# Layer 1 of a two-layer hybrid backbone entered by token tiles, low halves of weights moved in VectorE's order, step size sums in two runs

## The chip, the cores and the metric

The kernel runs on one core of a Trainium2 chip. The metric is the device time of one launch in microseconds, as the median of several runs.

## What is computed

The reference passes 256 latent tokens of width 2048 (and 256 context tokens) through two layers; everything is float32.

```
# layer 0: neighbourhood attention (16 heads of 128) beside a bidirectional SSD scan (8 groups)
shift, scale, gate = split(silu(c) @ ada_w[0] + ada_b[0])
h = rms_norm(x, g[0]) * (1 + scale) + shift          # the context likewise
p = h @ w_in                                         # 2048 x 14400
ya = attention(q, k, v, context) * silu(gate columns)
yb = gated_group_rmsnorm(ssd(x, dt, B, C) + d * x, z)
x = x + gate * (concat(ya, yb) @ w_out)              # 4096 x 2048
# layer 1: short gated convolution
h = rms_norm(x, g[1]) * (1 + scale1) + shift1
bg, cg, hv, g_ = split(h @ sc_w_in)                  # 2048 x 8192
x = x + gate1 * ((silu(g_) * bg * dw_conv(cg * hv)) @ sc_w_out)
```

Inside the scan the step sizes dt are summed along the tokens, forwards and backwards, over the latent tokens (two tiles of 128) and over the context.

## The kernel before

**Products.** Every large product is done in three passes of a shortened float32 format. A weight chunk of 128 x 1024 numbers is loaded into a `raw` buffer. Then `split` (L379) makes two parts of it: ScalarE casts it to the high half wH (L395), and VectorE subtracts that from the weight, which gives the low half wL (L396). There are three wH and three wL buffers, so the chunk that is split takes the place of the one three chunks back. The activations are kept in two parts, too (hH and hL, or one tile h that holds both side by side). TensorE multiplies high by high, low by high and high by low (L188 is the one line of all matmuls, L192 that of all transposes).

**Order.** The instructions of every engine run in the order in which they are written out, and that order is made by a planner at build time. `Plan` (from L38) keeps a modelled time for each engine and each tile. The main program writes TensorE's matmuls in order; after a few of them `pump` looks through three queues of tasks (`urgent`, `side`, `back`). A task is a generator that yields what it needs next (an engine and tiles), and `may` lets it go on once the modelled times say that its inputs are there. `splits_try` writes the next split as soon as the planner takes its weight to have landed, up to three chunks ahead of the one in use; while `hold` is set it writes none, and the queue `back` stands still. `issue` writes the next weight load on SP's queue when a raw buffer is free. A DMA on ScalarE's queue is modelled to end 1500 ns after its transfer.

**Layer 0.** For eight pairs of 128 input columns the modulation (`ada_gen`: products in TensorE, two transposes, the sums L697 to L703 on VectorE) yields h, while keys, values, queries and the first B columns are accumulated by `part_gen` (L749, L751). Then follow the rest of the input projection with attention heads (`head_gen`), the step sizes (`dt_gen`, L1045 to L1136) and the scan (`make_b`, `make_c`, `make_x`, `group_gen`). Meanwhile the task `gemv_gen` in the queue `back` works out further modulation rows on VectorE alone, in pairs of products over a loaded weight (L776).

In `dt_gen` the dt of both streams lies token by token in four blocks of 64 columns (32 heads, two directions). Fourteen matmuls with triangular or all-ones matrices add them up into one bank: running sums of the two latent tiles, their strict sums and totals, and the same for the context.

**Output projection and entry into layer 1.** The output projection goes over 16 chunks of `w_out` (two of the 32 blocks of mixed heads each) for column groups of 512: two groups together, then the third, then the fourth. Each group has a bank for either token tile (`ps[0]`, `ps[1]`), and in every chunk both tiles are multiplied in turn. `res_gen` (from L1491) takes a finished group: for either tile it multiplies the bank by the gate (L1506), adds the residual to give x1a or x1b (L1509) and squares that on ScalarE with a sum along the row (L1511). `turn_gen` (from L1524) transposes x1 block by block (16 blocks of 128 columns, two transposes each, one bank for a block) and scales it on ScalarE on its way to a `late` tile (L1534); blocks 0 to 7 come early, the others once the last group has passed. `norm_gen` (from L1538) starts when all four groups are done: it adds the sums of squares (L1540), takes the power -1/2 of both tiles on GpSimd (L528), builds two diagonal matrices (L1544) and spreads them over the partitions by matmuls into the bank `rb`. Then for each block: the product with `rb` (L1561), the high part on ScalarE (L1563) and the low part on VectorE (L1553). `hold` is set for the last of the 16 chunks of the last group and taken back when block 1 of layer 1 is ready.

**Layer 1.** 16 groups of four banks (`both`, `cg_gen`, `hv_gen`, `bg_gen`, `gg_gen`), each over eight chunks of `sc_in`; then the last projection, four groups of eight chunks of `sc_out`. Its inputs y are made in two parts by `gg_gen` (high L1667, low L1668).

Of the kernel before, what the change touches and what calls it, by code (L numbers as in the profile page):

```python
# [15 lines left out]
KB = 16  # L16
# [21 lines left out]
class Plan:  # L38
# [59 lines left out]
    def add(self, b):  # L98
# [10 lines left out]
        if op == "DMACopy":  # L109
# [4 lines left out]
            if e == "SP":  # L114
                self.dma = max(self.dma, s + 1000) + n / self.RATE
                done = free = self.dma + 1000
            else:
                done = free = max(self.dma, s + 1000) + n / self.RATE + 1500
# [23 lines left out]
def kernel(ctx: ExitStack, tc, x, cx, ada_w, ada_b, w_in, w_out, sc_in, sc_out, rpb, small, const,  # L142
# [96 lines left out]
    def may(task, hor, isurg):  # L239
# [5 lines left out]
        if nb and len(free_b) < nb + (0 if isurg else reserve[0]):  # L245
            return False
        now, t = plan.t["PE"], plan.t["ACT" if eng == "AQ" else eng]
# [130 lines left out]

    def split():  # L379
# [3 lines left out]
        if n == 64:  # L383

            W = WH[k % NW].rearrange("p (b c) -> p b c", b=nb)
# [9 lines left out]
        E(S.copy(H, v))  # L395
        E(V.tensor_tensor(out=Lo, in0=v, in1=H.bitcast(F32), op=ALU.subtract))  # L396
        HL[k] = (H, Lo)
        pos["split"] += 1
        give_raw(raw)
        issue()  # L400

# [17 lines left out]
    def splits_try():  # L419
        if hold[0]:  # L420
            return
        while pos["split"] < pos["use"] + NW and pos["split"] in RAW:
            if plan.ready([RAW[pos["split"]][1]]) > max(plan.t["PE"], plan.t["ACT"]) + 300:
                return
            split()

    def use(ahead=0):
        k = pos["use"] + ahead
        while pos["split"] <= k:
# [4 lines left out]
            split()  # L434
        splits_try()
# [609 lines left out]
    def dt_gen(ps):  # L1045
# [52 lines left out]
        first = True  # L1098
# [32 lines left out]
        E(V.tensor_copy(rw[:64, 0:256], pr[:64, :256]))  # L1131
        E(S.activation(rw[:64, 256:512], pr[:64, :256], AF.Exp))
# [358 lines left out]
    def res_gen(k, c0, ps):  # L1491
# [10 lines left out]
        yield when(lambda: x1 and k in passed)  # L1502
        for t in range(2):
            gb, xr = g2[t]
            yield W_("DVE", ps[t], gb)
# [3 lines left out]
            E(V.tensor_tensor(out=x1[t][:, cols], in0=gb, in1=xr, op=ALU.add))  # L1509
            yield W_("ACT", x1[t][:, cols])  # L1510
            E(S.activation(xr, x1[t][:, cols], AF.Square, accum_out=ss1[:, t, k:k + 1]))  # L1511
            give(free_t, gb, xr)
# [245 lines left out]
```

## Time and profile before

| | us |
|---|---|
| median of 3 runs | 1822.08 |
| lowest and highest | 1821.28, 1822.44 |
| profiled execution | 1820.64 |
| its span, first to last instruction | 1818.9 |
| first TensorE instruction after | 13.8 |
| busy DVE (VectorE) | 1259.2 |
| busy ACT (ScalarE) | 777.4 |

The names in the profile: PE is TensorE's matmuls, PEld its weight loads, DVE is VectorE, ACT ScalarE, POOL GpSimd, SP the queue of loads. A row of the timeline reads: start, length (both us), engine, line, operation, output <- inputs, partitions x elements, count of instructions merged, and in brackets the idle time just before and what ended it. Matmuls overlap, so a row of 0.39 us doesn't mean that the next one waits so long: at full clock the next 512-column matmul starts 0.23 us later. A row of the waits reads: engine, line and tile <- what it waited for: total us, times, longest.

### The profile page before, as it was taken

Reading aid. Unit: us, or ns where it says so; the run is one execution under the profiler, and the core shown is the slowest. Engines: PE = TensorE matmul, PEld = TensorE weight load, DVE = VectorE, ACT = ScalarE, POOL = GpSimd, SP = SyncE. Lnnn points to the kernel's source line nnn. Section 1 sums busy time; section 2 is a strip of 40 time slices with the busy share of each in tenths; the row PEclk is TensorE's granted clock in tenths of the full one; section 3 lists DMA queues with packets and bytes.
Section 4 is the critical chain, followed back from the end, with each engine's and each line's share of the span. In section 5 each row is a group of like instructions: output and inputs, shape, how many; then the busy total and the mean of one; then the engine's idle time right before and its main releaser. Section 6 shows DMA issues by size and latency. Waiting matters only on the chain.

```text
span 1818.9 us, 26339 instructions
## 1 busy us (share of the span) xinstructions
PE 1785.2 (98%) x9959; PEld 1488.2 (82%) x9959; DVE 1259.2 (69%) x2039; ACT 777.4 (43%) x1369; POOL 28.5 (2%) x27
## 2 busy tenths in 40 slices
PE   6999999999999999999999999999999999999998
PEld 4677988888888888888887898788878888888877
DVE  5566785877575877565877677776567777776655
ACT  5323443445232454232444443654444444444442
POOL 0000100000000001000001000000000000000000
PEclk9999999999999999999999999999999999999999
DMA  9997644576565566545575557678676777777665
GB/s 330 334 299 256 203 132 131 167 223 178 169 185 191 154 199 182 192 139 177 163 225 162 169 146 246 206 226 289 220 243 209 222 251 228 231 248 221 186 203 156
DMA packets 249216, 376.90 MB, mean 207 GB/s; under 512 B 32656, under 2 KB 104048, under 8 KB 249088
## 3 DMA queue, kind: packets, MB, share of 16 engines
q1 hardware_dynamic: 239792, 366.64, 65.4%
q10 hardware_dynamic: 9296, 8.57, 1.4%
q8 instruction: 78, 1.28, 0.3%
q14 instruction: 50, 0.41, 0.1%
HBM read 368.70 MB, written 7.77 MB: 207 GB/s over the span
## 4 chain that ended last, share of the span: by engine, by line
PE 84%; issue 8%; DVE 2%; DMA 1%; ACT 1%; POOLq 0%; POOL 0%; SPq 0%; ACTq 0%; DVEq 0%
PE bank L188 82%; PE bank L192 2%; DVE wL L396 1%; DMA raw<-in_ada_w 1%; DMA tmp<-dram_csr 1%; ACT wH L395 0%; DVE tmp L1150 0%; DVE acc L776 0%; DVE h L1553 0%; DVE tmp L1331 0%; DVE hL L725 0%; DVE tmp L1691 0%; DVE tmp L721 0%; DVE tmp L1689 0%; DVE tmp L1334 0%
## 5 line engine op out<-in xcount | busy, mean ns | idle before, releaser
L395 ACT CAST wH<-raw 128x1024 fp32r<-128x1024 f32 (+1 forms) x439 | 458.4, 1046 | 730.4 <-PE bank L188 582.8
L396 DVE TENSOR_TENSOR wL<-raw,wH 128x1024 fp32r<-128x1024 f32 (+1 forms) x439 | 533.0, 1217 | 336.0 <-ACT wH L395 329.6
L188 PE MATMUL bank<-h,wH 128*128 128x512 f32 x1024 | 360.9, 398 | 2.0 <-DVE h L1553 2.0
L188 PE MATMUL bank<-hH,wH 128*128 128x256 f32 (+1 forms) x1040 | 353.4, 340 | 0.8 <-ACT wH L395 0.8
L188 PE MATMUL bank<-hL,wH 128*128 128x256 f32 (+1 forms) x1040 | 338.6, 326 | 0.0
L188 PE MATMUL bank<-hH,wL 128*128 128x256 f32 (+1 forms) x1024 | 331.7, 324 | 0.3 <-DVE wL L396 0.3
L188 PE MATMUL bank<-h,wL 128*128 128x256 f32 x1024 | 286.4, 280 | 0.4 <-DVE wL L396 0.4
L188 PE MATMUL bank<-wH,hH 128*128 128x512 f32 x640 | 257.9, 403 | 3.9 <-ACT hH L719 2.6
L188 PE MATMUL bank<-wL,hH 128*128 128x512 f32 x640 | 250.6, 392 | 0.0
L188 PE MATMUL bank<-wH,hL 128*128 128x512 f32 x640 | 249.7, 391 | 0.1
L188 PEld LDWEIGHTS bank<-h,wH 128*128 128x128 f32 x1024 | 193.0, 188 | 49.6 <-DVE h L1553 2.5
L776 DVE SCALAR_TENSOR_TENSOR acc<-raw,csil,acc 128x512 f32<-128x512 f32 x256 | 191.9, 750 | 42.7 <-DMA raw<-in_ada_w 37.7
L188 PEld LDWEIGHTS bank<-hH,wH 128*128 128x128 f32 x1040 | 196.8, 189 | 24.3 <-issue 7.4
L188 PEld LDWEIGHTS bank<-hL,wH 128*128 128x128 f32 x1040 | 197.1, 190 | 19.7 <-issue 4.8
L188 PEld LDWEIGHTS bank<-hH,wL 128*128 128x128 f32 x1024 | 194.2, 190 | 18.0 <-DVE wL L396 1.0
L188 PEld LDWEIGHTS bank<-h,wL 128*128 128x128 f32 x1024 | 193.5, 189 | 0.7 <-DVE wL L396 0.7
L188 PE MATMUL bank<-wH,mix 128*128 128x512 f32 x512 | 164.1, 396 | 0.3 <-ACT Vt L945 0.3
L188 PEld LDWEIGHTS bank<-wH,hH 128*128 128x128 f32 x640 | 120.2, 188 | 35.4 <-issue 6.2
L188 PEld LDWEIGHTS bank<-wH,hL 128*128 128x128 f32 x640 | 120.2, 188 | 26.3 <-DVE hL L725 0.6
L188 PEld LDWEIGHTS bank<-wL,hH 128*128 128x128 f32 x640 | 120.2, 188 | 24.7 <-DVE wL L409 0.5
L188 PEld LDWEIGHTS bank<-wH,mix 128*128 128x128 f32 x512 | 96.1, 188 | 22.3 <-issue 1.7
L188 PE MATMUL bank<-wL,mix 128*128 128x512 f32 x256 | 99.9, 390 | 0.0
(241 smaller groups left out, 1663.9 us busy)
## 6 DMA issues: line engine op xcount, KB each, us to landing
raw<-in_w_in SPq DMA_DIRECT2D x210, 512.0 KB
raw<-in_ada_w SPq DMA_DIRECT2D x162, 512.0 KB
raw<-in_sc_in SPq DMA_DIRECT2D x128, 512.0 KB
raw<-in_w_out SPq DMA_DIRECT2D x64, 512.0 KB
raw<-in_sc_out SPq DMA_DIRECT2D x32, 512.0 KB
tmp<-dram_csr SPq DMA_DIRECT2D x32, 256.0 KB
PT<-in_ada_w SPq DMA_DIRECT2D x14, 512.0 KB
xtm<-in_ada_w SPq DMA_DIRECT2D x9, 512.0 KB
```

The costliest lines, as they stand in the source:

```text
L188: E(T.matmul(o, l, r, start=start, stop=stop, skip_group_check=True))
L192: E(T.transpose(o, i, ident if k == 128 else ident[:k, :k]))
L395: E(S.copy(H, v))
L396: E(V.tensor_tensor(out=Lo, in0=v, in1=H.bitcast(F32), op=ALU.subtract))
L776: E(V.scalar_tensor_tensor(out=acc, in0=v[:, j], scalar=csil[:, 2 * k + j:2 * k + j + 1], in1=acc, op0=ALU.mult, op1=ALU.add))
```

## The change

1. `split` writes only the cast on ScalarE and puts the low half on a list, `lows`. `low_part` writes the subtraction later: as soon as the planner takes the cast to be done by the time at which VectorE (or TensorE) has come (`lows_try`, which is called ahead of every VectorE task that is let go and around every split), or at the latest when the chunk is used. The raw buffer is given back, and the next load written, with the low half.
2. In the last column group the last three chunks (13 to 15) are multiplied token tile by token tile: all 18 matmuls of the first tile, then all 18 of the second. Splits and the queue `back` are held from chunk 13 on. `res_gen` goes on with the first tile when its rows are done.
3. `norm_gen` is started before these matmuls. It adds the first three groups' sums beforehand, and takes power, diagonal and broadcast for each tile by itself; between the power and the diagonal of the first tile it splits one weight. `keep_up` writes transposes of the identity whose results nobody reads: eight behind the last transposes of x1, six behind the broadcast of the second diagonal.
4. `turn_gen` transposes two blocks into one bank. Blocks 8 to 13 stay in their three banks until VectorE scales and multiplies them in one instruction there; from block 4 on the broadcast is read from a copy (`r2`) in place of the bank `rb`. Two weights are split at blocks 1 and 3.
5. In `dt_gen` eight matmuls take the place of fourteen, by treating two blocks of 64 columns in one, and adding totals through the all-ones matrix; other work of about 2.5 us (planned) is let in between the first four and the last four.
6. The planner takes DMAs on ScalarE's queue to end 2500 ns after their transfer, and one task waits for a copy that it did not name before.

```diff
@@ split
+    lows = deque()
     def split():
...
         E(S.copy(H, v))
-        E(V.tensor_tensor(out=Lo, in0=v, in1=H.bitcast(F32), op=ALU.subtract))
-        HL[k] = (H, Lo)
+        lows.append((k, H, Lo, v, raw))
         pos["split"] += 1
-        give_raw(raw)
-        issue()
+    def low_part():
+        k, H, Lo, v, raw = lows.popleft()
+        E(V.tensor_tensor(out=Lo, in0=v, in1=H.bitcast(F32), op=ALU.subtract))
+        HL[k] = (H, Lo)
+        give_raw(raw)
+        issue()
+    def lows_try():
+        while lows and not hold[0] and plan.ready([lows[0][1]]) <= max(plan.t["PE"], plan.t["DVE"]) + 200:
+            low_part()
@@ dt_gen
-        for t in range(2):
-            mm(pc[:, t, f], U, dam[:, t, f], first, True)
-            first = False
-            mm(pc[:, t, b], L, dam[:, t, b], False, True)
-        for d_, i in ((f, 0), (b, 1)):
-            mm(pc[:, 2, d_], sS2[:, i, :], dam[:, i, d_], False, True)
-            mm(pc[:, 3, d_], ONES, dam[:, i, d_], False, True)
-        for t in range(2):
-            for d_, i, other in ((f, 0, 1), (b, 1, 0)):
-                has2 = t != other
-                mm(pc[:, 4 + t, d_], sS2[:, i, :], dam[:, 2 + t, d_], False, not has2)
-                if has2:
-                    mm(pc[:, 4 + t, d_], ONES, dam[:, 2 + other, d_], False, True)
+        mm(pc[:, 0:2, f], U, dam[:, 0:2, f], True, True)
+        mm(pc[:, 0:2, b], L, dam[:, 0:2, b], False, True)
+        for i, d_, lo in ((0, f, 0), (1, b, 1)):
+            mm(pc[:, 2, d_], sS2[:, i, :], dam[:, lo, d_], False, True)
+        t0 = plan.t["PE"]
+        yield when(lambda: plan.t["PE"] > t0 + 2500)
+        for i, d_ in ((0, f), (1, b)):
+            mm(pc[:, 4:6, d_], sS2[:, i, :], dam[:, 2:4, d_], False, True)
+        for d_, o, q in ((f, slice(3, 5), slice(0, 4, 3)), (b, slice(3, 6, 2), slice(1, 3))):
+            mm(pc[:, o, d_], ONES, dam[:, q, d_], False, True)
@@ turn_gen
+        for kp in range(0, KB, 2):
+            yield when(lambda: ("x1", kp // 4) in got and (kp < 8 or len(passed) == 4))
...
+            if kp == 14:
+                keep_up(8)
+                yield when(lambda: ("sq", 3, 1) in got)
+            for b in range(2):
+                kb = kp + b
+                if kp < 8 or kp == 14:
+                    yield W_("ACT", pt)
+                    E(S.activation(late[kb], pt[:, b * 256:(b + 1) * 256], AF.Copy, scale=A1[:, kb:kb + 1]))
+                else:
+                    held[kb] = pt
+    def keep_up(n):
+        pt = bank()
+        for _ in range(n):
+            turn(pt[:, :128], ident)
+        give(free_b, pt)
@@ norm_gen
+        for t in range(2):
+            dt_ = dg[:, t * 128:(t + 1) * 128]
+            yield when(lambda: ("sq", 3, t) in got)
+            yield W_("DVE", ss1[:, t])
+            r = r1[:, t:t + 1]
+            E(V.tensor_scalar(out=r, in0=ss1[:, t, 3:4], scalar1=s3[:, t:t + 1], scalar2=1.0 / D, op0=ALU.add, op1=ALU.mult))
+            E(G.tensor_tensor(out=r, in0=r, in1=mhalf[:, :1], op=ALU.pow))
+            ahead = t == 0 and pos["split"] < pos["use"] + NW and pos["split"] in RAW
+            if ahead:
+                split()
+            yield W_("DVE", r1[:, t:t + 1])
+            E(V.tensor_scalar(out=dt_, in0=ident, scalar1=r1[:, t:t + 1], scalar2=None, op0=ALU.mult))
+            if ahead:
+                while lows:
+                    low_part()
+            yield W_("PE", dt_, nb=0 if t else 1)
...
+            mm(rb[:, t * 128:(t + 1) * 128], ONES, dt_, t == 0, True)
+        keep_up(6)
...
+            if kb not in held:
+                E(V.tensor_tensor(out=late[kb], in0=late[kb], in1=rb[:, :256] if r2 is None else r2, op=ALU.mult))
+            else:
+                E(V.scalar_tensor_tensor(out=late[kb], in0=held[kb][:, (kb % 2) * 256:(kb % 2) * 256 + 256], scalar=A1[:, kb:kb + 1],
+                                         in1=r2, op0=ALU.mult, op1=ALU.mult))
...
+            while lows and kb in (3, 5):
+                low_part()
+            if kb == 3:
+                r2 = half()
+                E(S.copy(r2, rb[:, :256]))
+                give(free_b, rb)
+            if kb in (1, 3) and pos["split"] < pos["use"] + NW and pos["split"] in RAW:
+                split()
@@ output projection
+    NTAIL = 13
-            hold[0] = len(passed) == 3 and ip == 15
+            hold[0] = len(passed) == 3 and ip >= NTAIL
+            if hold[0]:
+                if ip > NTAIL:
+                    continue
...
+                ws = [use(q) for q in range(16 - NTAIL)]
+                spawn(urgent, norm_gen(), 0, 1)
+                for t in range(2):
+                    for q, (H, Lo) in enumerate(ws):
+                        for b in range(2):
+                            i = 2 * order[NTAIL + q] + b
+                            mm_act([pss[0][t]], mH[i][:, 0, t * 128:(t + 1) * 128], mH[i][:, 1, t * 128:(t + 1) * 128],
+                                   H[:, b], Lo[:, b], False, NTAIL + q == 15 and b == 1)
+                        if t:
+                            used()
+                    got.add(("rows", 3, t))
+                    pump()
+                continue
```

In the order of the changed build TensorE's instructions are the same as before up to the first modulation products behind the queries of the second column pair (about 78 us in the profile); VectorE's differ from the split at 66.22 us on.

More of the change, by code (lines that the diff above doesn't have):

```diff
@@ L425, in splits_try @@
             split()
+            lows_try()
     def use(ahead=0):
@@ L1538, in norm_gen @@
+    def keep_up(n):
+        pt = bank()
+        for _ in range(n):
+            turn(pt[:, :128], ident)
+        give(free_b, pt)
+    s3 = st([128, 2], "s3")
     def norm_gen():
-        yield when(lambda: len(done) == 4)
-        E(V.tensor_reduce(out=r1, in_=ss1, axis=AX.X, op=ALU.add))
-        rstd(r1, r1, D, EPS, 2)
+        yield when(lambda: all(("sq", k, 1) in got for k in range(3)))
+        yield W_("DVE", ss1)
+        E(V.tensor_reduce(out=s3, in_=ss1[:, :, 0:3], axis=AX.X, op=ALU.add))
+        E(V.tensor_scalar(out=s3, in0=s3, scalar1=D * EPS, scalar2=None, op0=ALU.add))
@@ L1556, in low @@
             h1[kb] = hls[kb].rearrange("p a b -> p (a b)")
+        base = pos["use"]
+        r2 = None
         for kb in range(KB):
-            yield when(lambda: ("turn", kb) in got)
-            yield W_("DVE", rb, late[kb])
-            E(V.tensor_tensor(out=late[kb], in0=late[kb], in1=rb[:, :256], op=ALU.mult))
+            yield when(lambda: ("turn", kb) in got and (kb < 6 or pos["use"] >= base + kb // 2 - 2))
+            yield W_("DVE", rb if r2 is None else r2, held[kb] if kb in held else late[kb])
+            if kb not in held:
[3 more added lines that the diff above has]
+                                         in1=r2, op0=ALU.mult, op1=ALU.mult))
+                if kb % 2:
+                    give(free_b, held[kb])
             hls[kb] = st([128, 2, 256], f"hL{kb}", F32R, name=f"h1_{kb}")
```

45 lines of the change are left out of this document (25 added, 20 removed).

## The prediction

> **What bounds the kernel now.** I read the page first, then busy time by stretch, then what TensorE waited for, and last the timeline of the three places where it waited. The page:
>
> ```profile
> span 1818.9 us, 26339 instructions
> ...
> PE 1785.2 (98%) x9959; PEld 1488.2 (82%) x9959; DVE 1259.2 (69%) x2039; ACT 777.4 (43%) x1369; POOL 28.5 (2%) x27
> ```
>
> TensorE is busy 98% of the span, so an edit pays only if it removes TensorE work or one of its 33.7 us of idle time. The table by stretch says where that idle time lies (length, then busy time and count of PE, its weight loads, DVE, ACT and POOL, then granted clock, DMA share and GB/s):
>
> ```profile
> 0.00:75.00 75.00, 53.78 (x388) 36.40 (x389) 42.38 (x111) 37.36 (x80) 2.93 (x10) 1.00 1.03 340
> 75.00:1353.00 1278.00, 1276.62 (x7088) 1063.44 (x7086) 892.86 (x1478) 527.94 (x991) 24.90 (x16) 1.00 0.65 197
> 1353.00:1386.00 33.00, 28.07 (x151) 23.34 (x150) 25.27 (x50) 19.82 (x36) 0.70 (x1) 0.95 0.42 133
> ```
>
> From 75 to 1353 us TensorE misses 1.4 us in all: there the change can lose, but hardly win. The start misses 21 us, the entry into layer 1 (1353 to 1386) 5 us at a lowered clock, and one more wait comes at the last projection. The sum goes through these three and one removal of work.
>
> **The start.** The builds keep TensorE's order until about 78 us, ScalarE's as long and VectorE's until the weight split at 66.22. So all waits before it stay. Then:
>
> ```profile
> 65.53 0.38 PE L192 MATMUL bank<-const,half 128*128 128x128 f32 x2
> 66.22 1.23 DVE L396 TENSOR_TENSOR wL<-raw,wH 128x1024 fp32r<-128x1024 f32 x1 [3.94 <-ACT wH L395]
> 67.95 0.17 DVE L697 TENSOR_REDUCE S<-bank 128x4 f32<-128x16 f32 x1
> 69.48 0.69 DVE L725 TENSOR_TENSOR hL<-tmp,hH 128x512 fp32r<-128x512 f32 x1 [0.39 <-ACT hH L719]
> 71.54 0.68 DVE L751 TENSOR_TENSOR gt<-gt,bank 128x512 f32<-128x512 f32 x1
> 72.27 0.50 PE L188 MATMUL bank<-wH,hH 128*128 128x512 f32 x1 [1.16 <-DVE gt L751]
> ```
>
> The low half stands in VectorE's queue and waits there for ScalarE's cast, with the shift sums (L697) behind it, though the transposes that they read were done at 65.53 + 0.38 = 65.91. In the changed order the low half comes behind these sums: L697 runs at 65.95, the low half follows, then the same instructions as before up to gt. Before, gt stood 3.59 us behind L697. Now the low half lies between (1.14 us from one start to the next, by the split rows below), and the wait of 0.39 us for hH goes, since ScalarE is free early: 65.95 + 3.59 + 1.14 - 0.39 = 70.29, and gt frees its bank near 71.0. Before, TensorE waited 1.16 us for it, from 71.1 on, and lost 0.1 in the restart. I take the whole stall, **-1.3 us**. The ends are 0 (the gain is lost at the next DMA; the DMA share is 1.03 here) and -1.3.
>
> **The step size sums** are 14 matmuls, which the trace records as 28 passes:
>
> ```profile
> 264.60 0.97 PE L188 MATMUL bank<-half,const 128*128 128x32 f32 x8
> ...
> 267.42 0.39 PE L188 MATMUL bank<-half,const 128*128 128x32 f32 x2
> ```
>
> 26 passes lie between the starts of the first and the last two: 2.82 / 26 = 0.108 us each, 0.217 a matmul. The change has 8 matmuls instead, six of them with 64 columns. A 64-column pass is not in the trace; it costs at least as much as the 32-column one and, as the 128-column transposes of the entry go at 0.11 us, no more than that. So six matmuls less are **-1.3 us** of TensorE work, in a stretch where TensorE has no idle time. Parting them into two runs puts some 2.5 us of other matmuls between them. The sums, their exponentials, the two DRAM writes on ScalarE's queue and whatever stands behind them in VectorE's queue come that much later. I cost it at nothing: the sums end near 268, and the first product that uses them (wst) comes at 335.3:
>
> ```profile
> L1229 DVE TENSOR_TENSOR tmp<-bank,wst x32: 415/417/422, 335.3 to 1109.2; 128x256 f32<-128x256 f32 x32
> ```
>
> Were that cover gone, it would be those 2.5 us.
>
> **The entry into layer 1.** The last rows matmul of layer 0 starts at 1353.22; the first of layer 1 at 1360.56, 7.34 us later:
>
> ```profile
> 1353.22 0.39 PE L188 MATMUL bank<-wH,mix 128*128 128x512 f32 x1
> 1355.20 0.69 DVE L1509 TENSOR_TENSOR x1b<-tmp,tmp 128x512 f32<-128x512 f32 x1
> 1356.66 0.27 PE L192 MATMUL bank<-const,x1b 128*128 128x128 f32 x1
> 1357.13 0.70 POOL L528 TENSOR_TENSOR r<-r,const 128x2 f32<-128x2 f32 x1 [143.48 <-DVE r L527]
> 1359.02 0.75 DVE L1561 TENSOR_TENSOR PT<-PT,bank 128x256 f32<-128x256 f32 x2 [0.67 <-PE bank L188]
> 1360.56 0.79 PE L188 MATMUL bank<-h,wH 128*128 128x512 f32 x1 [1.57 <-DVE h L1553]
> 1363.28 0.63 PE L188 MATMUL bank<-h,wH 128*128 128x512 f32 x1
> 1363.91 0.40 PE L188 MATMUL bank<-h,wH 128*128 128x512 f32 x1
> 1379.79 0.38 PE L188 MATMUL bank<-h,wL 128*128 128x256 f32 x1 [0.42 <-DVE wL L396]
> 1381.66 0.50 PE L188 MATMUL bank<-h,wH 128*128 128x512 f32 x1 [0.43 <-DVE h L1553]
> ```
>
> Three losses are to be seen. The chain x1b, square, power, diagonal, broadcast, first block is 7.34 us. The first five pairs of layer 1 take 3.35 us (1360.56 to 1363.91) at slow rows (0.63 against 0.40); five pairs at the later pace of 1.39 us for four take 1.74, so 1.6 us are lost. Two stalls follow (0.42 and 0.43 us idle, about 1.2 us with the restart).
>
> The changed order, counted from T, the start of the last rows matmul. The first token tile's rows end 18 matmuls (4.1 us) earlier, so x1a, its square, its own power and diagonal lie beside the second tile's matmuls. In VectorE's order one low half (1.22 us) stands between that diagonal and x1b; it ends near T + 1.0, where x1b could have begun at T + 0.62. So x1b is multiplied and added by T + 2.35 (before: 1355.89, T + 2.67). TensorE then does 15 transposes at 0.11 us (two took 0.38 at 65.53, one takes 0.27 here) to T + 4.1 and eight added ones to T + 4.9, and only then the broadcast of the second diagonal. That diagonal is ready near T + 4.2. Before, 1.24 us lay between x1b's end and the power, two sums among them; with one of them gone (0.2) the power starts at T + 3.4. On one column it takes 0.55 us by this row, and the diagonal 0.3:
>
> ```profile
> L528 POOL TENSOR_TENSOR rx<-rx,const x4: 548/554/564, 8.5 to 40.1; 128x1 f32<-128x1 f32 x4
> ```
>
> So the fillers cost 0.7 us of the chain. VectorE's first product starts at T + 5.3 (before: 1359.02, T + 5.80), and layer 1 1.54 us behind it as before, at T + 6.84: 0.5 us gained.
>
> If the clock holds, another 1.6 us fall away, but not all of it stays, since VectorE has to keep the pace:
>
> ```profile
> 1369.05 2.36 DVE L396 TENSOR_TENSOR wL<-raw,wH 128x1024 fp32r<-128x1024 f32 x2 [1.12 <-ACT wH L395]
> 1371.33 0.41 DVE L1561 TENSOR_TENSOR xtm<-xtm,bank 128x256 f32<-128x256 f32 x1
> 1371.66 0.48 DVE L1553 SCALAR_TENSOR_TENSOR h<-xtm,M,h 128x256 fp32r<-128x256 f32 x1
> 1372.06 0.41 DVE L1561 TENSOR_TENSOR xtm<-xtm,bank 128x256 f32<-128x256 f32 x1
> ```
>
> A pair of blocks costs VectorE two products, two low parts (0.73 us a block from one L1561 to the next) and one split (1.14 us, as 2.36 is for two and 1.22 for one): 2.6 us, against 2.78 us of TensorE. Six blocks now read their product from a held bank by a form that the trace doesn't show; between the 0.41 and the 0.48 of these rows I take 0.48. And where before splits were held back only from the last chunk of rows, with two weights of layer 1 split by then, the hold now begins two chunks earlier and one is split; one more split of 1.14 us comes after the entry. Going through the order of both queues with these rows, TensorE waits some 0.1 us at blocks 2 and 4, 0.3 and 0.75 at blocks 6 and 7 (two splits in a row ahead of block 7's low part) and 0.45 at block 11: 1.6 us, against 2.8 us (clock and stalls) before. The entry as a whole: 0.5 + 1.2 = **-1.7 us**. One end is -4.0 (no stall in layer 1, and no 0.7 us for the fillers). The other is +2: the last rows chunk's low half stands behind a pair of L776 in VectorE's queue, whose longest wait for DRAM is 3.8 us (row below); some 3.5 of it would reach TensorE.
>
> The trace's own clock row is the 0.63 against 0.40, after idle pieces of at most 1.57 us. [...]
>
> **The last projection**:
>
> ```profile
> 1744.64 0.40 ACT L1667 CAST y<-v 128x256 fp32r<-128x256 f32 x1
> 1744.77 1.22 DVE L396 TENSOR_TENSOR wL<-raw,wH 128x1024 fp32r<-128x1024 f32 x1 [0.63 <-ACT wH L395]
> 1745.91 0.42 DVE L1668 TENSOR_TENSOR y<-v,y 128x256 fp32r<-128x256 f32 x1
> 1746.38 0.74 PE L188 MATMUL bank<-wH,y 128*128 128x512 f32 x2 [0.56 <-DVE y L1668]
> ```
>
> In the changed order y's low part stands ahead of that split. What it subtracts is cast by 1745.04, so it ends near 1745.5. TensorE waited 0.56 us for it and lost 0.1 in the restart: **-0.7 us** (0 to -0.7).
>
> **All other splits** change places with VectorE's neighbours. What they stood in the way of:
>
> ```profile
> DVE wL L396 <- ACT wH L395: 333.5, 247, 4.6
> ...
> DVE acc L776 <- DMA raw<-in_ada_w: 37.7, 33, 3.8
> ```
>
> VectorE loses 333.5 us in its queue to ScalarE's cast, but TensorE pays for next to none of it between 75 and 1353, so I put these at 0. What covers a later low half is its slack:
>
> ```profile
> 1346.58 1.23 DVE L396 TENSOR_TENSOR wL<-raw,wH 128x1024 fp32r<-128x1024 f32 x1 [1.50 <-ACT wH L395]
> 1350.93 1.05 ACT L395 CAST wH<-raw 128x1024 fp32r<-128x1024 f32 x1 [1.66 <-PE bank L188]
> ```
>
> With three buffers the cast at 1350.93, for which TensorE had to leave a chunk, marks where TensorE begins with the weight of the first row; its low half is done at 1347.81: 3.1 us to spare, more than any one VectorE instruction. The ends are -1.4 (all idle time of that stretch) and +9 (the second rival). The planner's longer latency for writes on ScalarE's queue adds no instruction; 0, with the same ends.
>
> **Sum**: 1.3 + 1.3 + 1.7 + 0.7 = 5.0 us. The profiled execution took 1820.64 us (span 1818.9 and 1.7 around it), which would become 1815.6; the median of the runs shown is 1.4 us higher, 1822.08, so I forecast **1817.1 us**.
>
> **Rivals.** *The entry gives nothing* (0.24): the clock drops in the 2 us before x1b, or VectorE's pace eats what the clock gains. For: VectorE needs 2.6 of every 2.78 us and starts one split behind. Against: the 14 fillers keep TensorE going for 1.5 us just before the first block. Then 5.0 - 1.7 = 3.3 us are left: 1818.8.
>
> *Low halves late, slower* (0.14): a low half that is put off stands behind a product of L776 that waits for its weights from DRAM. 33 such waits are in the trace, up to 3.8 us. A pair of L776 (1.53 us) and a wait use up the 3.1 us of slack when the wait is over 1.6 us: that is the point from which it decides. The longest would stall TensorE by 2.2 us. If a third of the 33 stalled it by 0.8, it would be 9 us: 1822.1 - 5.0 + 9 = 1826. Against: the mean wait is 1.1 us, and the planner puts a low half ahead of any VectorE work that would start after its cast.
>
> *More than the sum* (0.10): the new order also removes the small waits of the middle (1.4 us) and the entry's later stalls (1.6): 5.0 + 3.0 = 8.0, so 1814.1.
>
> **How the numbers follow.** The forecast has 0.52. About 0.2% (3.6 us) is what a measurement of this kernel can tell from no change: under 1818.4 counts as faster. Forecast and third rival lie there, 0.62; the first rival is same, 0.24; the second slower, 0.14. The range leaves out the second rival and a little below the third: 1812.5 to 1822.5, which takes in the ends of the single terms but not all of them at once.
>
> **What would show it.** Right: no wait for gt at 70 us; the 28 passes become 16; layer 1 enters some 6.8 us behind the last rows matmul with rows of 0.40 from the start, and waits of VectorE in its first eleven blocks; no wait for y at the last projection. Wrong: rows of 0.63 in layer 1; idle TensorE between 75 and 1353 well over 1.4 us, released by wL; a wait for wL of the last rows chunk, whose split stands behind a pair of L776.

## The result, and the profile after

The changed kernel takes 1819.88 us in the median of 22 runs (1814.1 to 1822.41); the kernel before, run beside it, 1822.26. The ratio is 0.9982, with a 95% interval of 0.9974 to 0.9989: 3.3 us or 0.18% faster, within what I called the same. The forecast was 1817.1 us, a gain of 5.0. The profiled execution of the changed kernel took 1820.47 us, one of the longer half of its runs.

From the page of the changed kernel (span 1818.7 us), then two of the three stretches of the prediction, in the same columns:

```profile
PE 1784.1 (98%) x9961; PEld 1488.1 (82%) x9961; DVE 1259.5 (69%) x2041; ACT 775.2 (43%) x1364; POOL 32.4 (2%) x28
```

```profile
75.00:1353.00 1278.00, 1271.65 (x7081) 1059.31 (x7080) 910.53 (x1509) 526.71 (x990) 28.32 (x16) 1.00 0.67 203
1353.00:1386.00 33.00, 30.76 (x180) 26.13 (x179) 27.55 (x50) 20.04 (x35) 1.12 (x2) 1.00 0.47 150
```

In the middle TensorE now misses 6.35 us (1278.00 - 1271.65) where it missed 1.4. In the entry it misses 2.2 us in place of 4.9, and the clock there is 1.00 in place of 0.95.

I cut both traces, and later those of the experiments, at the same matmuls, found by their count among those over the same operands (us):

| stretch, up to | before | changed | difference |
|---|---|---|---|
| 601st matmul of the input projection (from the first matmul) | 191.62 | 192.12 | +0.5 |
| last rows matmul | 1147.81 | 1149.14 | +1.3 |
| start of layer 1's second group | 32.78 | 29.91 | -2.9 |
| last matmul of layer 1's last group | 338.16 | 340.18 | +2.0 |
| end | 94.69 | 93.63 | -1.1 |

So the profiled executions differ by 0.2 us, the medians by 2.4. The +2.0 us of layer 1's body lies within what the same instructions vary by (experiment 5).

**Start.** VectorE and TensorE of the changed kernel:

```profile
66.62 0.17 DVE L716 TENSOR_REDUCE S<-bank 128x4 f32<-128x16 f32 x1 [2.36 <-PE bank L192]
66.91 1.23 DVE L408 TENSOR_TENSOR wL<-raw,wH 128x1024 fp32r<-128x1024 f32 x1
71.68 0.50 PE L188 MATMUL bank<-wH,hH 128*128 128x512 f32 x1 [0.34 <-DVE gt L770]
...
86.65 1.23 DVE L408 TENSOR_TENSOR wL<-yi,wH 128x1024 fp32r<-128x1024 f32 x1
90.68 1.28 DVE L770 TENSOR_TENSOR sz<-sz,bank 128x512 f32<-128x512 f32 x2
91.42 0.51 PE L188 MATMUL bank<-wH,hH 128*128 128x512 f32 x1 [1.00 <-DVE sz L770]
```

The sums stand ahead of the low half, as forecast, and the wait for gt falls from 1.16 to 0.34 us. But at 91.42 there is a wait of 1.00 us that before had not. Before, a low half stood ahead of the same kind of addition, for the next column pair, too:

```profile
89.14 1.22 DVE L396 TENSOR_TENSOR wL<-yi,wH 128x1024 fp32r<-128x1024 f32 x1
90.28 1.28 DVE L751 TENSOR_TENSOR sz<-sz,bank 128x512 f32<-128x512 f32 x2
91.01 0.50 PE L188 MATMUL bank<-wH,hH 128*128 128x512 f32 x1
```

What is new is TensorE's order. Before, 24 projection matmuls stood between the shift transposes (85.06) and the matmul at 91.01; now there are 18, because six of them (1.4 us) were written ahead of the modulation products at 76.73. So TensorE comes to this place sooner than VectorE. From the transposes at 66 us to this matmul, with the same 81 projection matmuls between them, it takes 25.28 us in place of 25.49: of the 1.3 us at gt, 0.2 stay. The +0.5 us of the table arose earlier, up to those transposes (52.44 us from the first matmul, before 51.74), where the change does nothing yet; over all thirteen profiles of this document that part takes 51.48 to 52.48 us.

**Middle.** Waits of TensorE from 75 to 1353 us (engine, line and tile <- what it waited for: total us, times, longest); together 6.3 us, against 1.2 before:

```profile
PE bank L188 <- ACT Vt L964: 2.4, 1, 2.4
PE bank L188 <- DVE half L1374: 1.6, 3, 0.8
PE bank L188 <- DVE wL L408: 1.3, 2, 0.7
PE bank L188 <- DVE sz L770: 1.0, 1, 1.0
```

The longest by its timeline:

```profile
1162.42 1.07 ACT L1488 CAST mix<-tmp 128x256 fp32r<-128x256 f32 x3 [1.02 <-DMA tmp<-dram_mixd]
1162.86 1.43 DVE L1489 TENSOR_TENSOR mix<-tmp,mix 128x256 fp32r<-128x256 f32 x4 [1.35 <-ACT mix L1488]
...
1163.71 1.04 ACT L401 CAST wH<-raw 128x1024 fp32r<-128x1024 f32 x1
1164.21 0.42 DVE L1351 TENSOR_TENSOR tmp<-tmp 128x256 f32<-128x256 f32 x1
1164.66 1.55 ACT L964 COPY Vt<-bank 128x512 f32<-128x512 f32 x3
...
1165.28 0.73 PE L188 MATMUL bank<-tmp,xtm 128*64 128x128 f32 x8 [2.42 <-ACT Vt L964]
```

A cast of mixed heads stands in ScalarE's queue and waits there for its read from DRAM; VectorE's low half of it (L1489) waits behind, and behind that L1351, whose result the scan's matmul needs, done at 1164.63. What ended the wait is later still: the first of ScalarE's three copies (L964), which stands behind the mixed heads and a weight's cast (L401). No wL is in this chain.

**Entry.** From the last rows matmul (1354.96) to the first of layer 1 it is 6.27 us (6.84 forecast, 7.34 before), and TensorE waits once in the first group:

```profile
1354.96 0.39 PE L188 MATMUL bank<-wH,mix 128*128 128x512 f32 x1
...
1358.02 1.04 PE L192 MATMUL bank<-const 128*128 128x128 f32 x8
1358.82 0.29 DVE L1598 TENSOR_SCALAR half<-const,r 128x128 f32<-128x128 f32 x1 [0.67 <-POOL r L1593]
1359.17 0.49 PE L188 MATMUL bank<-half,const 128*128 128x128 f32 x2
1361.23 0.50 PE L188 MATMUL bank<-h,wH 128*128 128x512 f32 x1 [0.92 <-DVE h L1611]
...
1371.88 0.47 PE L188 MATMUL bank<-h,wH 128*128 128x512 f32 x1 [0.49 <-ACT h L1630]
```

The second diagonal ends at 1358.82 + 0.29 = 1359.11, and its broadcast starts at 1359.17: the eight fillers ahead of it were just done.

**Last projection.** The low part of y goes ahead of the split, and TensorE no longer waits for it:

```profile
1745.98 0.42 DVE L1761 TENSOR_TENSOR y<-v,y 128x256 fp32r<-128x256 f32 x1 [1.46 <-ACT y L1760]
1746.32 1.22 DVE L408 TENSOR_TENSOR wL<-raw,wH 128x1024 fp32r<-128x1024 f32 x1
```

**A clock row that I had overlooked** lies behind the step size sums of the kernel before. The trace's clock is full or half in stretches of 3413 ns, and these lie on one grid: the halved stretches at 268.21 and at 1360.47 are 320.0 lengths apart. Before, by those stretches, then the first of them by the sums' own matmuls alone (busy time and count):

```profile
264.80:268.21 3.41, 3.41 (x30) 3.32 (x30) 1.21 (x6) 0.04 (x1) 0.00 (x0) 1.00 0.53 153
268.21:271.62 3.41, 3.41 (x11) 2.54 (x10) 3.24 (x11) 2.07 (x8) 0.00 (x0) 0.50 0.00 1
```

```profile
264.80:268.21 3.41, 3.01 (x27) 1.00 0.53 153
```

TensorE counts as busy all the time, but 27 narrow passes fill 3.01 of the 3.41 us, and the next stretch runs at half the clock: matmuls start 0.43 us apart (268.60, 269.02, 269.45) in place of 0.23, a loss of 3.41 x (1 - 0.23/0.43) = 1.6 us. In the changed kernel the clock there is 1.00:

```profile
268.00:272.00 4.00, 4.00 (x22) 3.10 (x21) 2.55 (x11) 0.88 (x4) 0.00 (x0) 1.00 0.31 116
```

So narrow passes did not hold the clock here, though TensorE's busy time was full. It is one case, but the other profiles bear it out: in all thirteen, every other halved stretch behind 60 us follows a stretch in which TensorE was idle for over a quarter of the time (ahead of the one at 1360.47 it was busy for 0.68 of the 3.41 us). And by the columns that they stream, at 0.23 us for 512, the matmuls from 264.80 to 268.21 come to some 0.8 us of work by my estimate; wherever else TensorE was busy for a whole stretch it was 1.1 us or more by the same count (1.1 from 15.62 us on in the kernel before), and the clock stayed full behind it.

The changed kernel has a halved stretch near the start, at 27.8 us, that before has not. It shows no price: the way to the transposes at 66 us takes 51.5 to 52.4 us in the nine profiles that have it and 51.7 to 52.5 in the four others.

### The profile page after: what moved, and what is told of

Read it like the earlier page. It is cut to its first block, busy times and chain, and to the rows that moved or that the text cites. A ratio compares the mean times of both kernels' runs of the same rounds, so it can differ in the third digit from the quotient of the medians.

```text
span 1818.7 us, 26323 instructions
## 1 busy us (share of the span) xinstructions
PE 1784.1 (98%) x9961; PEld 1488.1 (82%) x9961; DVE 1259.5 (69%) x2041; ACT 775.2 (43%) x1364; POOL 32.4 (2%) x28
## 5 line engine op out<-in xcount | busy, mean ns | idle before, releaser
L401 ACT CAST wH<-raw 128x1024 fp32r<-128x1024 f32 (+1 forms) x439 | 457.7, 1043 | 710.2 <-PE bank L188 556.2
L795 DVE SCALAR_TENSOR_TENSOR acc<-raw,csil,acc 128x512 f32<-128x512 f32 x256 | 191.9, 749 | 48.5 <-DMA raw<-in_ada_w 37.9
```

The costliest lines, as they stand in the source:

```text
L795: E(V.scalar_tensor_tensor(out=acc, in0=v[:, j], scalar=csil[:, 2 * k + j:2 * k + j + 1], in1=acc, op0=ALU.mult, op1=ALU.add))
```

## The experiments

Two theories at the outset. Theory 1, the prediction's: work removed and waits removed add up, and the other splits are free. Theory 2: the gains are in the clock and at the entry, and low halves in VectorE's order take back much of them in the middle. Every edit of a task makes the planner draw the order anew, so totals carry that draw; rows of single places decide. Ratios are to the kernel before, beside the same runs.

**1 to 3, the step size sums.** The kernel before with the eight new matmuls in two runs, with the eight in one run, and with the old fourteen parted behind the eighth. The first line stands for the eight (runs 1 and 2), the others part them (runs 1 and 3):

```diff
+        mm(pc[:, 0:2, f], U, dam[:, 0:2, f], True, True)
...
+        t0 = plan.t["PE"]
+        yield when(lambda: plan.t["PE"] > t0 + 2500)
```

> The kernel before with part 5 of the change alone: eight step size matmuls (16 passes) in two runs of four, in place of fourteen (28 passes) in one run. Theory A (work alone): the passes take 1.4 us less, 3.04 us to 1.6 us, and nothing else; the total falls by 1.4 us, and a half-clock stretch like the 268.2 to 271.6 us of before is a chance that this edit doesn't touch. Theory B (clock): the run of 28 narrow passes is what halves the granted clock for 3.41 us right behind it, which costs another 1.7 us; here the clock row of 260 to 276 us stays at 1.00, and the total falls by 3.1 us. The order of all later work is drawn anew by the planner, so that the total may miss either by 2 us; the clock row decides.

> The kernel before with the eight new step size matmuls, but in one run of 16 passes (about 1.6 us). It tells whether the clock goes by the length of the run of narrow passes or by the parting. Theory A (work alone): total -1.4 us, and the clock behind the run 1.00 or not by chance. Theory B: a run of 1.6 us is under half of the 3.41 us for which the clock was halved, so that I expect 1.00 behind it and -3.1 us; if the clock halves here too, then the parting is what saved it, and the total falls by 1.4 us only.

> The kernel before with the fourteen old matmuls, parted by some 2.5 us of other matmuls behind the first eight (16 passes, then 12). No work is removed. Theory A (work alone): 0 us, and the half clock behind the sums comes or not by chance. Theory B: neither run (1.7 and 1.3 us) is long enough, the clock row of 260 to 276 us stays at 1.00, and the total falls by 1.7 us. If parting itself costs (sums, exponentials and DRAM writes come 2.5 us later), there are waits of TensorE for a wst product or DA row near 335 us, which before doesn't have; I expect none.

Measured: 0.9990 (0.9982 to 0.9999), 0.9993 (0.9984 to 1.0002), 0.9995 (0.9986 to 1.0003), that is -1.8, -1.3 and -0.9 us. In all three the clock behind the sums stays at 1.00, of the fourteen parted in both stretches that hold them (263.86 to 267.27 and on to 270.68). The totals alone don't tell -1.4 from -3.0: two of these profiles have half-clock stretches elsewhere (1 and 3, near 955 us behind a wait), which cost back as much. Experiments 4 and 11 go on with it.

**4, low halves alone.** The kernel before with part 1 only.

> The kernel before with part 1 of the change alone: low halves written apart from the casts, in VectorE's order. By the prediction: the wait for gt at 72 us goes (-1.3 us), the wait for y at the last projection goes (-0.7 us), the rest 0: -2.0 us, with VectorE's waits for ScalarE's cast falling from 333 us to about 285 us. Theory that part 1 gives nothing: the waits for gt and y move to the next DMA or product, and new waits for wL or for bank copies behind low halves come in the middle: between -0.5 and +2 us. The half clock behind the step size sums (268 us) should stand as in the kernel before, as the sums are the old ones, and that at the entry into layer 1 too.

Measured: 1.0010 (1.0002 to 1.0019), 1.8 us slower. The wait for y went (end stretch 93.64 us, -1.05). The gain at gt came back as a loss in the same place as in the changed kernel (25.29 us from the transposes at 66 us to the matmul behind it, before 25.49). Waits from 75 to 1353 us, 3.2 us in place of 1.2:

```profile
PE bank L188 <- DVE wL L408: 2.2, 2, 1.7
PE bank L188 <- DVE sz L770: 1.0, 1, 1.0
```

Both are theory 2. But a new draw of the order alone can give as much: run 8 below, with low halves at once, has 3.3 us there. The wait for sz is in no run of that kind (see the table further down). And with the old sums in one run the clock held. Its stretch with most of the narrow passes, by the sums' own matmuls, and the stretch behind it, of all work:

```profile
266.77:270.18 3.41, 2.65 (x24) 1.00 0.54 154
```

```profile
270.18:273.59 3.41, 3.41 (x16) 2.41 (x15) 3.18 (x11) 2.11 (x6) 0.00 (x0) 1.00 0.00 0
```

So behind 3.01 us of narrow passes in one stretch the clock was halved, and behind 2.65 it was not: the same 28 passes, cut by the stretches at other places. The run of 28 passes lasts 3.21 us by the same view (264.60 to 267.42 + 0.39). Of the 3.41 us of places at which a stretch can begin, 0.60 (3.41 - 3.21 + 2 x 0.20) put at least 3.01 us of it into one stretch, and 1.32 (with 2 x 0.56) at least 2.65. So by this estimate, in which a stretch begins at every place as often as at any other (no run shows that), 18 to 39% of the executions of the kernel before lose the 1.6 us, 0.3 to 0.6 on average.

**5 and 6, the fillers.** The changed kernel without both runs of fillers, and without the eight alone (the same edit where n is 8):

```diff
     def keep_up(n):
-        pt = bank()
-        for _ in range(n):
-            turn(pt[:, :128], ident)
-        give(free_b, pt)
+        plan.t["PE"] += n * (128 / 1.2 + 3)
```

> The changed kernel without both runs of filler transposes (the eight behind the last transposes of x1 and the six behind the second broadcast); nothing else moves. My step said that the fillers cost 0.7 us of the chain into layer 1. Theory C (fillers hold the clock): without them TensorE has about 2 us without work beside x1b and 1.5 us more before the first block; the clock halves at the entry as in the kernel before (first pairs of layer 1 at rows of 0.63 us, clock row 1361 to 1364 near 0.5), and the total rises by 1.6 us, less at most 0.7 us. Theory D (fillers only cost or do nothing): the clock stays at 1.00, the six kept entry as fast as with them or faster by up to 0.7 us: total between -0.7 and 0.

> The changed kernel without the eight fillers behind the last transposes of x1; the six behind the second broadcast stay. If the eight lie on the chain to the second broadcast, that broadcast comes 0.7 us sooner behind the last rows matmul, and the total falls by 0.7 us; if the second diagonal is what the broadcast waits for (it started 0.35 us behind the last filler in the changed kernel's trace), the chain stays at 6.27 us and the total at 0. If the eight are needed for the clock, the first pairs of layer 1 go at half of it: +1.6 us.

Measured: 0.9998 (0.9989 to 1.0007) and 0.9987 (0.9978 to 0.9995), against 0.9982. The chain stays at 6.27 us in both: the fillers cost nothing on it. And the clock drops. From 1361 to 1365 us, in the changed kernel and on to 1386, then without any fillers, then without the eight:

```profile
1361.00:1365.00 4.00, 3.77 (x21) 3.31 (x22) 3.80 (x9) 3.52 (x7) 0.00 (x0) 1.00 0.00 0
1365.00:1386.00 21.00, 20.43 (x116) 17.37 (x115) 19.26 (x33) 12.68 (x20) 0.00 (x0) 1.00 0.60 194
```

```profile
1361.00:1365.00 4.00, 3.94 (x14) 3.37 (x15) 3.79 (x8) 3.34 (x6) 0.00 (x0) 0.60 0.02 3
```

```profile
1361.00:1365.00 4.00, 4.00 (x15) 3.43 (x15) 3.79 (x8) 3.04 (x6) 0.00 (x0) 0.57 0.13 16
```

Theory C is right on the mechanism: without both runs of fillers the clock is halved, and without the eight alone, too. But the first group gets longer by 0.2 and 0.6 us only (23.64 to 23.87 and 24.24), not by 1.6: TensorE, slower there, no longer waited for VectorE, and the idle 0.57 us from 1365 to 1386 is gone (busy for 21.00 of 21.00 us in both runs). The total of run 5, 2.9 us above the changed kernel's, is more than its profile shows; that profile is of its shortest run, and what the others lost is open.

That run also shows what layer 1's body is worth. 80 us of it, at full clock, changed and without fillers (whose instructions there are those of the changed kernel, in the same order); PE's count is in the first bracket:

```profile
1580.00:1660.00 80.00, 80.00 (x454) 69.36 (x454) 50.37 (x70) 37.82 (x56) 0.00 (x0) 1.00 0.63 188
```

```profile
1580.00:1660.00 80.00, 80.00 (x463) 70.00 (x462) 51.92 (x73) 38.65 (x57) 0.00 (x0) 1.00 0.65 190
```

463 or 454 matmuls in the same time with no wait: TensorE ran at one of two paces there, 22.19 or 22.61 us for a group of 64 pairs, and changed it only where eight small matmuls of a modulation row came between (in the kernel before, at 1415.1, 1496.0, 1578.6 and 1662.3 us). The body took 335.07 us in run 5 and 340.18 in the changed kernel. So a single execution says little to within 5 us, and the +2.0 us of the table can be such a draw. Whether the pace is set anew in each execution, one profile of each kernel can't show.

**7, the planner's constant.** The changed kernel with 1500 in place of 2500 ns.

> The changed kernel with the planner's old 1500 in place of 2500 ns for DMAs on ScalarE's queue (part 6 undone). I costed part 6 at 0. Rival: the 2.42 us wait for a bank at 1162.5 us, which before didn't have in this size (0.48 us), comes from where part 6 puts the mix cast on ScalarE's queue ahead of its DRAM read; then it is gone here and the total falls by 2.4 us. Against it: 2500 lets tasks wait longer for DRAM, not shorter, so that undoing it should make such waits more and longer: 0 to +2 us. Its order differs from about two thirds of the input projection on.

Measured: 0.9965 (0.9951 to 0.9978, six runs), 3 us under the changed kernel. But its profile has as many waits in the middle: 6.7 us, of them 3.4 for wL, 2.3 for half and 1.0 for sz. The stretch up to the last rows matmul is 1.9 us longer (1151.08) than in the changed kernel; the gain of this execution lies in layer 1's body (335.33 us), that is, in the pace. Why the median of six runs is lower stays open. The wait near 1163 is still there, as one for wL of 2.8 us: the constant didn't make it.

**8, low halves at once.** The changed kernel with part 1 undone:

```diff
         lows.append((k, H, Lo, v, raw))
         pos["split"] += 1
+        low_part()
```

> The changed kernel with part 1 undone: each low half is written right behind its cast, as before, and the entry and the step size sums stay as changed. By my sum part 1 is worth 2.0 us (gt wait at 70 us 1.3, y wait 0.7): the total rises by 2.0 us, the two waits are back, and the entry keeps its chain of 6.3 us and its full clock. If the entry also lives on part 1 (low halves held back until its own stalls are over), waits for wL or for h in the first twelve blocks of layer 1 come on top: +3 us. If the wait of 2.4 us at 1162 us comes from part 1, it goes here, and the total stays within 0.5 us.

Measured: 1.0020 (1.0011 to 1.0028), 6.9 us above the changed kernel. The chain is kept (6.33 us, clock 1.00), but the first group takes 30.57 us in place of 23.64. Its first products:

```profile
1361.67 1.22 DVE L409 TENSOR_TENSOR wL<-raw,wH 128x1024 fp32r<-128x1024 f32 x1 [0.85 <-ACT wH L401]
...
1362.82 0.41 DVE L1624 TENSOR_TENSOR PT<-PT,bank 128x256 f32<-128x256 f32 x1
...
1363.77 0.47 PE L188 MATMUL bank<-h,wH 128*128 128x512 f32 x1 [1.22 <-ACT h L1631]
```

VectorE waits 0.85 us for the cast with the next block's product behind it, and TensorE pays 1.2 us; this comes seven times. So beside the other parts, part 1 is worth 6.9 us at this place, which no term of my sum held. Alone it is worth nothing there: the first group of run 4 takes 25.45 us, as before.

**9 and 10, low halves put off only from the last column group on.** The changed kernel, then the same with 1500:

```diff
         pos["split"] += 1
+        if not defer[0]:
+            low_part()
...
             hold[0] = len(passed) == 3 and ip >= NTAIL
+            defer[0] = len(passed) == 3
```

> The changed kernel with low halves written right behind their casts up to the last column group of the output projection, and put off in VectorE's order only from there on. Theory E (part 1 pays at the entry and the last projection, and costs in the middle): TensorE's waits from 75 to 1353 us fall from 6.3 us (sz at 90 us, half, wL, the bank at 1163 us) to some 2 us, as they were 1.3 us in the kernel before and 3.4 us with part 1 undone, of which 1.3 us stood at the last chunk of rows; the wait for gt at 72 us comes back (1.2 us in place of 0.3); entry (6.3 us from the last rows matmul, first group 23.6 us) and last projection (no wait for y) stay as in the changed kernel. Total 3 us under the changed kernel, so some 0.9965 of before. Theory F (the middle is whatever the planner draws, whichever rule places the low halves): waits in the middle stay at 3 to 7 us in other places, and the total within 1.5 us of the changed kernel, 0.998 of before.

> As the run before it, and with the planner's 1500 in place of 2500 ns for DMAs on ScalarE's queue. If the constant is worth what the changed kernel with 1500 showed in total (0.9965 against 0.9982 of before, 3 us), the total falls by another 3 us, to 0.995 of before. If that gain was layer 1's pace (that run's profile has its waits in the middle at 6.7 us, no fewer than the changed kernel, and layer 1 behind its first group at 335.3 us against 340.2), the constant is worth 0 +- 1.5 us, by the draw of the order.

Measured: 0.9962 (0.9950 to 0.9975) and 0.9963 (0.9950 to 0.9975), 6.9 and 6.7 us under before: number 9 at 1815.65 us beats the kernel before and, over five runs, the changed one, though the two intervals just touch. Its waits from 75 to 1353 us:

```profile
PE bank L188 <- DVE tmp L1354: 1.3, 2, 0.6
```

1.3 us in place of 6.3. Up to the last rows matmul it takes 1146.12 us (-3.0 against the changed kernel), the entry 29.80, the end 93.62, as there. The wait for gt is back, and the one at 91 us is gone:

```profile
72.56 0.50 PE L188 MATMUL bank<-wH,hH 128*128 128x512 f32 x1 [1.15 <-DVE gt L773]
```

From the transposes at 66 us to that matmul it takes 25.43 us, 0.15 more than with the gain at gt: when either wait goes, the other takes most of its place. This is theory E. Number 10 shows the constant at 0 in total. But its profile doesn't repeat the gain in the middle: 3.0 us of waits, of which one for tmp near 955 us has 2.6, with a half-clock stretch behind it, and 1149.29 us up to the last rows matmul, as long as in the changed kernel; a faster pace in layer 1's body (336.25 us) makes up for it. So of the 3.0 us of number 9 a part can be a lucky order, and theory F falls only for the places that the table further down lists.

**11, the old sums in the changed kernel.** The fourteen matmuls in one run, the rest as changed.

> The changed kernel with the old step size sums, fourteen matmuls in one run (part 5 undone). Work alone: +1.4 us. With the clock: the run of 28 narrow passes halves the granted clock for 3.41 us behind it in this order too, +3.1 us; in the kernel with part 1 alone it did not, with the same 28 passes, so that a full clock here would say that the phase of a window decides, not the run by itself. Middle otherwise redrawn, +-2 us.

Measured: 1.0004 (0.9994 to 1.0013), 4.0 us above the changed kernel. The clock behind the run of 28 passes is full here, too, and a boundary of the stretches falls into the run (268.66):

```profile
268.66:272.07 3.41, 3.41 (x20) 2.81 (x20) 2.37 (x10) 1.85 (x7) 0.00 (x0) 1.00 0.30 115
```

The rest of the 4.0 us beyond the passes' 1.4 is not taken apart; in the profile, redrawn order shows as a wait for tmp of 1.0 us more, and as a half-clock stretch at 1170 us behind the wait that ends at 1169.

## Why the prediction was right, and where it was wrong

The time fell into the range, and the sign was right, but that is in part luck: the sum of 5.0 us was put together from terms that were off on both sides. The measured 3.3 us are just what the first rival (the entry gives nothing) would have left, and yet its mechanism did not occur: the entry gave more than any other place.

- **Start, -1.3: wrong.** The wait for gt shrank as forecast, and 0.2 us came of it. The step that failed is "I take the whole stall": it stopped at gt and didn't follow TensorE to the next pair, where a wait for sz of 1.00 us took its place. TensorE's order, which I took to stay until about 78 us, was redrawn around it. My end of 0 was right, by another wait than the DMA that I named.
- **Step size sums, -1.3: right on the work, short of the clock.** The four 64-column passes below start 0.095 us apart (four in 0.38), a little under my lower bound of 0.108, which I had taken from the narrower passes; 1.4 us of work went. The profiled execution lost another 1.6 us to the halved clock, which stood in the table of clocks and which I didn't look up, since TensorE was busy there. Over many executions that is worth 0.3 to 0.6 us by my estimate (run 4). Parting cost nothing that these runs can tell (run 3: -0.9 us).

```profile
265.94 0.55 PE L188 MATMUL bank<-half,const 128*128 128x64 f32 x4
266.32 0.58 PE L188 MATMUL bank<-half,half 128*128 128x32 f32 x4
```

- **Entry, -1.7: right in kind, mis-sized.** It gave 2.9: 1.07 from the chain (0.5 forecast; the fillers, which I charged 0.7, cost nothing, as the diagonal came no sooner) and 1.8 in the first group (1.2 forecast; I counted 1.6 us of waits in its blocks, and there is one of 0.49). The reason that I gave for the latter was wrong: run 5 enters at half clock as before did and still takes 23.87 us against 25.44. So the new order of work there is worth 1.2 to 1.6 (runs 6 and 5) and the clock the remaining 0.2 to 0.6; parts 2 to 4 were not told apart. And the whole stands on part 1 beside them: with low halves at once the entry loses 6.9 us.
- **Last projection, -0.7: right**: 0.8 at the place itself, with its restart; the end stretch is 1.1 us shorter, the rest of it in small steps without a wait.
- **All other splits, 0: the step that failed most.** I looked at the slack of the low halves themselves (3.1 us), and named wL as the releaser to look for. The waits grew by 5.1 us to 6.3, of which wL has 1.3; the rest is released by sz, half and Vt, which stand behind other work once the order is redrawn. That the putting off does it, and not any new order, shows in the same places of all thirteen profiles. With low halves at once in the middle are before and runs 1, 2, 3, 8, 9 and 10; with low halves put off there are the changed kernel and runs 4 to 7 and 11 (us):

| TensorE's wait | at once (7) | put off (6) |
|---|---|---|
| for gt near 72 | 1.12 to 1.16 | 0.34 to 0.35 |
| for sz near 91 | none | 0.99 to 1.00 |
| for wL near 212 | none | 0.34 to 0.82 |
| longest one near 1165 | none to 0.31 | 1.69 to 2.80 |
| longest one near 955 | 0.40 to 2.60 | none to 0.98 |
| all from 75 to 1353 | 1.2 to 3.3 | 3.2 to 7.2 |

  The row near 955 is the planner's draw, and it goes the other way. With the new sums, the stretch from the 601st to the last rows matmul takes 1144.91 to 1149.29 us at once (runs 1, 2, 8, 9, 10; mean 1147.2) and 1149.14 to 1151.07 put off (changed, 5, 6, 7; mean 1149.8): some 2.6 us by this estimate, beside a spread of 4.4 us among the first five alone.
- **The planner's constant, 0: right** in total, by runs 9 and 10; run 7's gain is not explained by its waits.

By the places: +0.5 at the start; -1.4 of passes, -1.6 of clock and +4.1 of waits (5.1 less sz, which lies in the start) up to the rows, which makes +1.1 where 1.3 was measured; -2.9 at the entry and -1.1 at the end. With the measured 1.3 these are -2.2 us without layer 1's pace, beside -2.4 between the medians and -3.3 by the ratio; the +0.5 and the -1.6 are draws of these two executions. The second rival, low halves late, was right that the putting off costs in the middle; some 4 of its 9 us came in this profile. But its mechanism, a low half behind a product of `gemv_gen` (L776 before, L795 now) that waits for DRAM, shows at one place, for 0.6 us; the cast of that chunk had been done at 208.47:

```profile
209.76 1.54 DVE L795 SCALAR_TENSOR_TENSOR acc<-raw,csil,acc 128x512 f32<-128x512 f32 x2 [4.00 <-DMA raw<-in_ada_w]
211.22 1.22 DVE L408 TENSOR_TENSOR wL<-raw,wH 128x1024 fp32r<-128x1024 f32 x1
212.49 0.38 PE L188 MATMUL bank<-hH,wL 128*128 128x256 f32 x1 [0.62 <-DVE wL L408]
```

## What to carry to other kernels

A stall that goes is only a gain if the next wait of the same engine doesn't grow by it: follow the engine to the next place where it waits, and past it. An order that helps at one place may be given to that place alone: low halves put off only from the last column group on kept the gain at the entry and left out the waits at 91, 212 and 1165 us. The totals (6.9 us against 3.3) don't prove it by themselves, as run 7, with low halves put off everywhere, gained 6.4. Read the clock stretch by stretch even where the engine is 100% busy, and don't trust a single execution to within its own draw of paces.

## What was not expected of the hardware

- The granted clock was halved for whole stretches of 3413 ns (at 268.21 and 1360.47 us in the kernel before), or for two, 6827, at the entry of runs 1 to 4. In the one case seen with TensorE 100% busy, narrow passes had filled 3.01 us of the stretch ahead; behind 2.65 us of them (run 4) the clock stayed full.
- In layer 1 the same matmuls ran at 22.19 or at 22.61 us a group, both at full clock; the pace changed only at the small matmuls of a modulation row (four times in the kernel before). This makes 5 us between two profiles with the same instructions in layer 1 (the changed kernel and run 5). What sets it was not found.
